# First FFN blocks in one written order: product 5 in halves around product 6, banks taken in turn, the next block's first product inside the down product

## The chip, the cores and the metric

One core of a Trainium2 chip runs the kernel. The metric is the device time of one execution in microseconds (us). The engines: PE is TensorE (matmuls), DVE is VectorE, ACT is ScalarE, POOL is GpSimd, SP is SyncE, which issues the loads. Each has its own queue of instructions and waits for semaphores of the others.

## The reference

One layer on x (512 rows, width 1024) and a memory of 256 rows, all in float32:

```
x = x + 1/2 * SwiGLU(RMSNorm(x))                       # FFN1: d_ff 2816
h = RMSNorm(x)
A, B, C = columns of h @ W_in:
   A: differential attention, 4 heads, rotary, block-causal
   B: chunked band attention, 8 heads, own chunk + 8 before, relative bias
   C: cross-attention into the memory:
      mk, mv = split(RMSNorm(mem) @ W_mem_kv)          # 256 x 512 each
      mk = RMSNorm per head(mk); cq = RMSNorm per head(cq)
      o_c = softmax(cq mk^T / sqrt(128)) mv
y = sum_i sigmoid(h W_g + b_g)_i * (o_i W_branch_i)
x = x + y W_out
x = x + 1/2 * SwiGLU(RMSNorm(x))                       # FFN2
x = RMSNorm(x)
SwiGLU(h) = (silu(h @ wg) * (h @ wu)) @ wd
```

## The kernel before

Each float32 product is made of three matmuls on operands split into a high part (a cast on ACT, L77, tiles with `hi` or `h` at the end) and a low part (a subtraction on DVE, L78, `lo` or `l`): high x high, low x high, high x low.

An FFN runs over the 22 tiles of d_ff in blocks of 4, 6, 6 and 6 (`CHUNKS`, L39). Within a block an `Item` is a pair of tiles. Its gate and up product for two tiles and two halves of the rows are computed by seven products instead of eight, in the manner of Strassen and Winograd: product p multiplies one of seven combinations of the four weight blocks (`prep`, L390) with one of seven combinations of the activations (`M[1]` to `M[7]`, made by `Operands.combine` and `need`, L205 to L242). A product is 24 matmuls of 256 columns (`mm7`, L364: two parts j, four k, three pairs of high and low). Products 1, 6, 7 and 4 add up in a bank of PSUM with the tag "s", products 5 and 3 in one with "p" or "o", product 2 has a bank "g". After products 1, 6 and 7 the state of the "s" bank is copied by ACT (`snap`, L417), since the next product of that chain adds to the same bank; `plus` (L422) adds such a copy to another bank on DVE (tile `cc`), `gated` makes silu(gate) x up (tile `pr`, L433), and `done` splits `pr` into `gh` and `gl`, the operands of the down product.

The weight combinations are DVE subtractions (`quarter` from `wraw`, L399, L400, L405, L409); `block` splits each into a ring of six buffer pairs: four `whi`/`wlo` and the two pairs `fhi`/`flo` and `ohi`/`olo`. So DVE and ACT make an operand pair for each product, while the first block also makes the seven activation operands (`mhi`/`mlo`).

After the products of a block comes its down product, in two halves of the columns (dh = 0 and 1); each has four banks, one for each 128 rows, and nf/2 pieces of 24 matmuls of 512 columns (`mm3`, L110 to L112). The last two products of the block, 4' and 3', stand between the first and the second piece of dh 0. (A prime stands for a block's second item.)

What sets the order: `run_jobs` (L334) prepares jobs ahead by a ring of six and runs each job's matmuls in a schedule of its own for PE; a scheduler places the jobs, and everything on DVE, ACT, POOL and SP. In the first block the order asked for is 1, 2, 1', 2', 6, 5, 7, 4, 3, 6', 5', 7', then the first down piece, 4', 3'. What PE got can be seen in the change's section.

Between the FFNs the mixer runs. Its cross-attention part makes the memory's keys: a product in two banks "s", a norm per head (`norm4`, with `mk` in L602) and transposes in bank "t" (`heads_T`, L615) into `mkh`/`mkl`; then `cq`, and then the values `mv`, again in two banks "s" (L651). In the mixer `PLAN_C0` and its likes are written rows that mix the steps of attention with pieces of other products. The banks in all: s 2, g 2, p 1, o 1, t 2 (L54).

## Time and profile before

| | us |
|---|---|
| median of 3 timed runs | 1266.1 (1265.81 to 1266.46) |
| the profiled execution | 1268.73 |
| its span | 1266.9 |
| PE busy | 1228.1 (97%) |
| DVE busy | 843.0 (67%) |
| ACT busy | 596.8 (47%) |
| PE in the chain that ended last | 91% |

The times of rows below are of the profiled execution, counted from the start of its span. Busy shares over the span hide stages; each row is read from the stage where it stands. The granted clock (PEclk) of 1.00 is 2.4 GHz, 0.50 is 1.2 GHz.

### The profile page before, as it was taken

The numbers are of one execution on the slowest core, as the hardware profiler recorded it, in microseconds if no ns is written. First come the engines' busy times: TensorE is split into PE (matmuls) and PEld (weight loads), VectorE is DVE, ScalarE is ACT, GpSimd is POOL, SyncE is SP. The second block draws the span as 40 slices with busy tenths as digits, with TensorE's granted clock in tenths as the row PEclk, the third lists the DMA queues.
The fourth block names the chain that finished last, engine by engine and source line by source line (L and its number), as shares of the span: only waits on it lengthen the run. The fifth ranks groups of instructions, "written<-read, shape, count | busy, mean of one in ns | idle before, by whom it ended". The sixth has DMA issues, their size and how long they took to land.

```text
span 1266.9 us, 19640 instructions
## 1 busy us (share of the span) xinstructions
PE 1228.1 (97%) x7808; PEld 1119.2 (88%) x7808; DVE 843.0 (67%) x1377; ACT 596.8 (47%) x1115; POOL 106.2 (8%) x108
## 2 busy tenths in 40 slices
PE   7889999999999899999999999999989999999997
PEld 7779989989987799999999999888887998998996
DVE  7977667667664756667765664554697776766753
ACT  7534525435443455554554544442464452542543
POOL 1100000000000301111121121111000000000002
PEclk8899999999999899999999999999989999999999
DMA  6532423323333413212221321145143242332311
GB/s 222 174 103 82 135 84 107 127 79 122 102 123 117 123 39 109 88 42 84 88 88 54 93 88 38 63 146 186 34 135 115 70 134 97 101 125 76 123 44 67
DMA packets 53084, 127.57 MB, mean 101 GB/s; under 512 B 10112, under 2 KB 10624, under 8 KB 52992
## 3 DMA queue, kind: packets, MB, share of 16 engines
q1 hardware_dynamic: 52416, 125.27, 31.1%
q8 instruction: 61, 1.00, 0.3%
q10 hardware_dynamic: 576, 1.05, 0.2%
q14 instruction: 31, 0.25, 0.1%
HBM read 122.11 MB, written 4.19 MB: 100 GB/s over the span
## 4 chain that ended last, share of the span: by engine, by line
PE 91%; DVE 4%; ACT 1%; DMA 1%; POOL 1%; issue 1%; SPq 0%; POOLq 0%; DVEq 0%; ACTq 0%
PE ps_s L373 19%; PE ps_g L110 9%; PE ps_g L112 9%; PE ps_g L111 9%; PE ps_o L373 5%; PE ps_p L110 5%; PE ps_p L112 5%; PE ps_p L111 4%; PE ps_p L373 4%; PE ps_g L373 4%; PE ps_s L110 3%; PE ps_s L111 3%; PE ps_s L112 3%; PE ps_o L906 2%; PE ps_s L874 2%; PE ps_t L722 1%
## 5 line engine op out<-in xcount | busy, mean ns | idle before, releaser
L77 ACT CAST whi<-wraw 128x1024 fp32r<-128x1024 f32 (+1 forms) x120 | 119.1, 993 | 144.6 <-PE ps_s L373 74.1
L78 DVE TENSOR_TENSOR wlo<-wraw,whi 128x1024 fp32r<-128x1024 f32 (+1 forms) x120 | 137.9, 1151 | 67.8 <-ACT whi L77 65.1
L373 PE MATMUL ps_s<-mhi,whi 128*128 128x256 f32 x496 | 140.3, 283 | 8.1 <-ACT snap L417 7.9
L373 PE MATMUL ps_s<-mlo,whi 128*128 128x256 f32 x496 | 139.3, 281 | 0.0
L373 PE MATMUL ps_s<-mhi,wlo 128*128 128x256 f32 x496 | 138.3, 281 | 0.6 <-DVE wlo L78 0.6
L373 PEld LDWEIGHTS ps_s<-mhi,whi 128*128 128x128 f32 x496 | 94.6, 191 | 10.6 <-ACT snap L417 9.5
L77 ACT CAST whi<-quarter 128x1024 fp32r<-128x1024 f32 x54 | 56.8, 1052 | 96.4 <-PE ps_o L112 22.4
L373 PEld LDWEIGHTS ps_s<-mlo,whi 128*128 128x128 f32 x496 | 94.7, 191 | 0.9 <-DVE mlo L78 0.2
L373 PEld LDWEIGHTS ps_s<-mhi,wlo 128*128 128x128 f32 x496 | 94.5, 191 | 0.9 <-DVE wlo L78 0.8
L110 PE MATMUL ps_p<-whi,hh 128*128 128x384 f32 (+1 forms) x264 | 95.0, 360 | 0.0
L112 PE MATMUL ps_p<-whi,hl 128*128 128x384 f32 (+1 forms) x264 | 89.6, 340 | 0.0
L111 PE MATMUL ps_p<-wlo,hh 128*128 128x384 f32 (+1 forms) x264 | 89.0, 337 | 0.0
L78 DVE TENSOR_TENSOR wlo<-quarter,whi 128x1024 fp32r<-128x1024 f32 x54 | 66.0, 1222 | 23.9 <-ACT whi L77 23.9
L110 PE MATMUL ps_g<-hh,fh 128*128 128x512 f32 x192 | 78.1, 407 | 0.0
L112 PE MATMUL ps_g<-hh,fl 128*128 128x512 f32 x192 | 75.5, 393 | 0.1
L111 PE MATMUL ps_g<-hl,fh 128*128 128x512 f32 x192 | 74.9, 390 | 0.0
L859 DVE CAST kx<-ps_t 128x256 fp32r<-128x256 f32 x32 | 13.6, 425 | 84.6 <-PE ps_t L857 84.6
L121 POOL TENSOR_TENSOR rsh<-msh,mhalf 128x4 f32<-128x4 f32 x38 | 45.2, 1191 | 277.5 <-DVE msh L127 225.8
L78 DVE TENSOR_TENSOR fl<-wraw,fh 128x768 fp32r<-128x768 f32 x48 | 50.0, 1042 | 24.0 <-ACT fh L77 24.0
L77 ACT CAST fh<-wraw 128x768 fp32r<-128x768 f32 x48 | 39.9, 833 | 37.7 <-PE ps_g L111 22.4
L724 ACT COPY pT<-ps_t 128x512 f32<-128x512 f32 (+3 forms) x56 | 23.5, 452 | 69.3 <-PE ps_t L722 69.3
L110 PEld LDWEIGHTS ps_p<-whi,hh 128*128 128x128 f32 x264 | 50.4, 191 | 1.6
(416 smaller groups left out, 3691.7 us busy)
## 6 DMA issues: line engine op xcount, KB each, us to landing
wraw<-in_ffn_w SPq DMA_DIRECT2D x88, 512.0 KB, 3.8
wraw<-in_ffn_wd SPq DMA_DIRECT2D x44, 512.0 KB, 3.9
wraw<-in_w_u SPq DMA_DIRECT2D x32, 384.0 KB, 3.2
wraw<-in_w_gb SPq DMA_DIRECT2D x32, 384.0 KB, 3.1
wraw<-in_w_gf SPq DMA_DIRECT2D x16, 384.0 KB, 3.1
wraw<-in_w_mem_kv SPq DMA_DIRECT2D x8, 512.0 KB, 4.1
wraw<-in_w_out SPq DMA_DIRECT2D x8, 512.0 KB, 4.8
x_sb<-in_x SPq DMA_DIRECT2D x4, 512.0 KB, 7.0
```

The costliest lines, as they stand in the source:

```text
L77: nc.scalar.copy(out=hi, in_=raw)
L78: (engine or nc.vector).tensor_tensor(out=lo, in0=raw, in1=f32(hi), op=ALU.subtract)
L110: nc.tensor.matmul(ps, lhsT=st[0], rhs=mv[0], start=first, stop=False)
L111: nc.tensor.matmul(ps, lhsT=st[0], rhs=mv[1], start=False, stop=False)
L112: return nc.tensor.matmul(ps, lhsT=st[1], rhs=mv[0], start=False, stop=last)
L121: nc.gpsimd.tensor_tensor(out=rs, in0=ms, in1=mhalf[:, :n], op=ALU.pow)
L373: nc.tensor.matmul(ps[:, c], lhsT=x, rhs=y, start=first and j + k + n == 0, stop=k == 3 and n == 2, skip_group_check=True)
L722: nc.tensor.transpose(ps[:, j * P:(j + 1) * P], pt[:, j * P:(j + 1) * P], ident)
L724: nc.scalar.copy(out=pT[:, :n * P], in_=ps[:, :n * P])
L859: nc.vector.tensor_copy(out=un.kx[:, :, qs], in_=heads(p2[:, 0:256], 2))
L874: nc.tensor.matmul(out_, lhsT=q, rhs=k, start=j == 0, stop=j == 1)
L906: nc.tensor.matmul(o[:, vs], lhsT=pT[:, j * P:(j + 1) * P], rhs=un.v[:, j, vs], start=j == 0, stop=j == i)
```

## The change

Both FFNs' first block gets one written order for PE. `run_jobs` opens one schedule for PE around all jobs of an FFN instead of one for each job, so that PE's matmuls stand in exactly the order of the list, over the blocks too. In the first block the list is now 1, 2, 1', 2', 5a, 6, 5b, 7, 6', 4, 3, 5', 7': product 5 is made in two halves (parts j = 0 and 1) around product 6. `prep` makes `s1` when the first of the products 5 and 6 needs it and `s4` after both. The first product of the second block is put at `hole`, after the products 4' and 3' within the first block's down product; the other blocks keep their lists. For dh = 1 the banks are taken in the order z, g, g, s instead of s, z, g, g. `G` (`gh`, `gl`) is made at its first use.

In the memory part the transposes of `mk` stand behind the product and the copies of `mv`, whose banks are "t" instead of "s"; `mk`, `mksq` and `cqsq` get tags of their own; `PLAN_C0` changes. `middle` is an argument that no call gives.

```
@@ run_jobs
-        for n, job in enumerate(jobs):
-            while made < len(jobs) and (made <= n or alive + jobs[made].blocks <= ring):
-                alive += jobs[made].blocks
-                jobs[made].got = jobs[made].prep() if jobs[made].prep else None
-                made += 1
-            with tc.manual_schedule(engines={mybir.EngineType.PE}):
+        with tc.manual_schedule(engines={mybir.EngineType.PE}):
+            for n, job in enumerate(jobs):
+                while made < len(jobs) and (made <= n or alive + jobs[made].blocks <= ring):
+                    alive += jobs[made].blocks
+                    jobs[made].got = jobs[made].prep() if jobs[made].prep else None
+                    made += 1
                 job.run(job.got)
-            alive -= job.blocks
+                alive -= job.frees
...
-        def mm7(ps, blk, m, first):
-            for j in range(2):
+        def mm7(ps, blk, m, first, parts=(0, 1)):
+            for j in parts:
...
+                if self.s1 is None:
+                    self.s1 = quarter()
+                    add(out=self.s1, in0=self.raw(2), in1=self.raw(3), op=ALU.add)
                 if p == 6:
-                    self.s1, self.s2 = quarter(), quarter()
-                    add(out=self.s1, in0=self.raw(2), in1=self.raw(3), op=ALU.add)
+                    self.s2 = quarter()
                     add(out=self.s2, in0=self.s1, in1=self.raw(0), op=ALU.subtract)
-                    return block(self.s2)
-                if p == 5:
-                    got = block(self.s1)
-                    self.s4 = quarter()
-                    add(out=self.s4, in0=self.raw(1), in1=self.s2, op=ALU.subtract)
+                    got = block(self.s2)
+                elif p == 5:
+                    got = self.blk5 = block(self.s1)
+                if p in (5, 6):
+                    self.done56 += 1
+                    if self.done56 == 2:
+                        self.s4 = quarter()
+                        add(out=self.s4, in0=self.raw(1), in1=self.s2, op=ALU.subtract)
                     return got
...
+                elif p == "5a":
+                    self.z = bank("p" if self.ft // 2 % 2 else "o")
+                    mm7(self.z, blk, 5, True, (0,))
+                elif p == "5b":
+                    mm7(self.z, self.blk5, 5, False, (1,))
...
+                order += [(items[0], "5a"), (items[0], 6), (items[0], "5b"), (items[0], 7), (items[1], 6), (items[0], 4),
+                          (items[0], 3), (items[1], 5), (items[1], 7)]
...
+                if n == 1:
+                    jobs.insert(hole, product(items[0], 1))
+                else:
+                    order += [(items[0], 1)]
...
-                    acc.extend(bank(t) for t in (("g", "g", "s", other) if dh == 0 else ("s", z, "g", "g")))
+                    acc.extend(bank(t) for t in (("g", "g", "s", other) if dh == 0 else (z, "g", "g", "s")))
...
                         if dh == 0 and k == 0:
                             jobs += end
+                            hole = len(jobs)
...
     for t in range(NMT):
-        yn = mem_pool.tile([P, 512], F32, tag="mk", name="mk", bufs=3)
-        sq = mem_pool.tile([P, 512], F32, tag="mk", name="mksq", bufs=3)
-        heads_T(norm4(mk_ps[t], yn, sq, gck), mkT, slice(t * P, (t + 1) * P))
+        yn = mem_pool.tile([P, 512], F32, tag="mk", name="mk", bufs=2)
+        sq = mem_pool.tile([P, 512], F32, tag="mksq", name="mksq", bufs=2)
+        mk.append(norm4(mk_ps[t], yn, sq, gck))
...
-    mv_ps = rows_product([bank("s") for _ in range(NMT)], mT, a["w_mem_kv"], 512, **mem_w)
+    mv_ps = rows_product([bank("t") for _ in range(NMT)], mT, a["w_mem_kv"], 512, **mem_w)
...
         nc.scalar.copy(out=mv[:, t, :], in_=mv_ps[t])
+    for t in range(NMT):
+        heads_T(mk[t], mkT, slice(t * P, (t + 1) * P))
...
-PLAN_C0 = "p2 c.qt p2 c.sc p2 f4 c.sc2 p3 f2 c.qt f2 c.pt f4 c.pv"
+PLAN_C0 = "p6 c.qt p3 f4 c.sc f4 c.sc2 f2 c.qt f1 c.pt f1 c.pv"
```

The first place is DVE in FFN1's first block. Before, with `flo_443` the low part of the operand of 6':

```order
L78 TENSOR_TENSOR mlo_65<-gl_126,mhi_64 128x1024
L141 SCALAR_TENSOR_TENSOR xn_3927<-mt_3917,rs_3925,gain_3888 128x512 x2
L78 TENSOR_TENSOR wlo_321<-quarter_318,whi_320 128x1024
L78 TENSOR_TENSOR wlo_361<-wraw_268,whi_360 128x1024
L399 TENSOR_TENSOR quarter_434<-wraw_436,wraw_438 128x1024
L78 TENSOR_TENSOR wlo_397<-quarter_282,whi_396 128x1024
L400 TENSOR_TENSOR quarter_435<-quarter_434,wraw_252 128x1024
L409 TENSOR_TENSOR quarter_509<-wraw_252,wraw_436 128x1024
L78 TENSOR_TENSOR olo_476<-quarter_434,ohi_475 128x1024
L422 TENSOR_TENSOR cc_543<-ps_o_483,snap_541 128x512
L405 TENSOR_TENSOR quarter_479<-wraw_258,quarter_435 128x1024
L78 TENSOR_TENSOR flo_443<-quarter_435,fhi_442 128x1024
```

In the changed kernel the low part for 6' is `wlo_361`:

```order
L439 TENSOR_TENSOR pr_424<-sg_425,cc_422 128x256
L78 TENSOR_TENSOR mlo_65<-gl_126,mhi_64 128x1024
L156 TENSOR_SCALAR ms_3638<-ss_3634 128x1
L78 TENSOR_TENSOR wlo_318<-quarter_315,whi_317 128x1024
L141 SCALAR_TENSOR_TENSOR xn_3642<-mt_3632,rs_3640,gain_3603 128x512 x2
L400 TENSOR_TENSOR quarter_352<-wraw_353,wraw_355 128x1024
L403 TENSOR_TENSOR quarter_358<-quarter_352,wraw_252 128x1024
L415 TENSOR_TENSOR quarter_491<-wraw_252,wraw_353 128x1024
L78 TENSOR_TENSOR olo_474<-quarter_352,ohi_473 128x1024
L411 TENSOR_TENSOR quarter_477<-wraw_258,quarter_358 128x1024
L428 TENSOR_TENSOR cc_523<-ps_o_434,snap_521 128x512
L78 TENSOR_TENSOR wlo_361<-quarter_358,whi_360 128x1024
```

Of the kernel before, `wlo_361` and `wlo_397`, the low parts for products 4 and 3, stand ahead of the low part for 6'. In the changed kernel they have left this place (product 4's follows behind, product 3's is a `flo` shortly ahead of this piece), and `pr` and `ms` have moved with the rows around them.

The second place is PE around the end of product 7 in FFN1's first block. Before, `ps_p_667` is 5', `ps_s_286` the first item's chain, here its products 7 (`whi_320`) and 4 (`whi_360`):

```order
L373 MATMUL ps_s_286<-mlo_65,whi_320 128x256
L373 MATMUL ps_s_286<-mhi_64,wlo_321 128x256
L373 MATMUL ps_p_667<-mhi_64,ohi_475 128x256
L373 MATMUL ps_p_667<-mlo_65,ohi_475 128x256
L373 MATMUL ps_s_286<-mhi_64,whi_360 128x256
L373 MATMUL ps_s_286<-mlo_65,whi_360 128x256
L373 MATMUL ps_s_286<-mhi_64,wlo_361 128x256
```

In the changed kernel `ps_s_284` with `whi_317` is product 7 and `ps_s_364` with `whi_360` product 6':

```order
L373 MATMUL ps_s_284<-mlo_65,whi_317 128x256
L373 MATMUL ps_s_284<-mhi_64,wlo_318 128x256
L373 MATMUL ps_s_364<-mhi_64,whi_360 128x256
L373 MATMUL ps_s_364<-mlo_65,whi_360 128x256
L373 MATMUL ps_s_364<-mhi_64,wlo_361 128x256
L373 MATMUL ps_s_364<-mhi_64,whi_360 128x256
L373 MATMUL ps_s_364<-mlo_65,whi_360 128x256
```

Where two matmuls of 5' and then product 4 followed product 7, product 6' follows it.

The third place is PE in the memory part. Before, `ps_s_4428` and `ps_s_4429` are the product for `mv`, and the transposes of the first `mk` (L615) stand between the two banks:

```order
L110 MATMUL ps_s_4428<-mwh_4450,mh_3886 128x512
L111 MATMUL ps_s_4428<-mwl_4451,mh_3886 128x512
L112 MATMUL ps_s_4428<-mwh_4450,ml_3887 128x512
L615 MATMUL ps_t_4232<-ident_80,mk_4221 128x128 x4
L110 MATMUL ps_s_4429<-mwh_4432,mh_3886 128x512
L111 MATMUL ps_s_4429<-mwl_4433,mh_3886 128x512
```

In the changed kernel the product for `mv` is in `ps_t_4129` and `ps_t_4130`, and the transposes (L638) of both `mk` and of the first `cq` (in `y_sb`) stand behind it:

```order
L110 MATMUL ps_t_4130<-mwh_4187,mh_3601 128x512
L111 MATMUL ps_t_4130<-mwl_4188,mh_3601 128x512
L112 MATMUL ps_t_4130<-mwh_4187,ml_3602 128x512
L638 MATMUL ps_t_4206<-ident_80,mk_3936 128x128 x4
L638 MATMUL ps_t_4213<-ident_80,mk_3947 128x128 x4
L638 MATMUL ps_t_4307<-ident_80,y_sb_4082 128x128 x4
L110 MATMUL ps_p_4286<-whi_4279,hh_3596 128x384
```

Three groups of transposes, in bank "t" as the product ahead of them, stand in a row.

## Rows read from the trace of the kernel before

**Rows 1.** Busy time by windows: us, then PE, PEld, DVE, ACT, POOL, clock, DMA, GB/s.

```profile
30.00:40.00 10.00, 5.67 (x27) 4.60 (x26) 9.56 (x12) 5.40 (x9) 4.86 (x1) 0.70 0.35 106
40.00:50.00 10.00, 8.46 (x57) 8.05 (x57) 9.56 (x12) 6.29 (x10) 1.39 (x1) 0.84 0.52 173
930.00:940.00 10.00, 9.68 (x63) 9.47 (x62) 10.00 (x12) 4.79 (x6) 0.00 (x0) 0.75 0.50 159
```

**Rows 2.** Waits of PE: releaser, us in total, times, longest.

```profile
PE ps_s L373 <- ACT snap L417: 7.9, 8, 1.5
PE ps_s L110 <- DVE mk L602: 5.8, 1, 5.8
...
PE ps_o L373 <- DVE mlo L78: 3.5, 2, 3.2
```

**Rows 3.** Busy time by windows, columns as in rows 1: stretches at half clock.

```profile
33.95:40.75 6.80, 5.16 (x21) 4.49 (x22) 6.36 (x9) 2.23 (x5) 0.93 (x1) 0.50 0.26 78
47.60:51.00 3.40, 3.40 (x18) 3.40 (x17) 3.40 (x4) 1.05 (x1) 0.00 (x0) 0.50 0.63 225
412.85:419.60 6.75, 4.68 (x11) 3.78 (x12) 4.72 (x10) 1.20 (x2) 2.60 (x3) 0.50 0.48 164
928.25:935.05 6.80, 6.20 (x29) 6.20 (x30) 6.80 (x9) 3.72 (x6) 0.00 (x0) 0.50 0.43 145
```

**Rows 4.** PE by time: start, us, line, operation, [idle before, releaser].

```profile
38.12 0.58 PE L373 MATMUL ps_o<-mlo,whi 128*128 128x256 f32 x1 [0.36 <-DVE mlo L78]
...
47.04 0.39 PE L373 MATMUL ps_s<-mhi,wlo 128*128 128x256 f32 x1 [0.62 <-DVE wlo L78]
...
414.92 0.77 PE L110 MATMUL ps_s<-mwh,mh 128*128 128x512 f32 x1 [5.78 <-DVE mk L602]
...
928.85 0.58 PE L373 MATMUL ps_o<-mlo,whi 128*128 128x256 f32 x1 [3.17 <-DVE mlo L78]
```

**Rows 5.** DVE by time, columns as in rows 4: first FFN, first block.

```profile
34.91 1.42 DVE L141 SCALAR_TENSOR_TENSOR xn<-mt,rs,gain 128x512 f32<-128x512 f32 x2 [0.44 <-POOL rs L121]
36.24 0.68 DVE L422 TENSOR_TENSOR cc<-ps_g,snap 128x512 f32<-128x512 f32 x1
36.84 1.22 DVE L78 TENSOR_TENSOR mlo<-gh,mhi 128x1024 fp32r<-128x1024 f32 x1
37.98 0.42 DVE L433 TENSOR_TENSOR pr<-sg,cc 128x256 f32<-128x256 f32 x1
...
40.05 1.22 DVE L78 TENSOR_TENSOR mlo<-gh,mhi 128x1024 fp32r<-128x1024 f32 x1
...
42.65 0.21 DVE L156 TENSOR_SCALAR ms<-ss 128x1 f32<-128x1 f32 x1
...
44.44 1.42 DVE L141 SCALAR_TENSOR_TENSOR xn<-mt,rs,gain 128x512 f32<-128x512 f32 x2 [0.44 <-POOL rs L121]
```

**Rows 6.** DVE by time: second FFN, first block.

```profile
921.30 1.22 DVE L78 TENSOR_TENSOR flo<-wraw,fhi 128x1024 fp32r<-128x1024 f32 x1
```

**Rows 7.** Chain that ended last, by time: start, us, what.

```profile
80.14 1.23 DVE wlo L78
...
84.14 0.50 PE ps_g L110
...
95.66 0.23 PE ps_g L111
...
100.98 2.83 PE ps_g L373 x24
...
989.31 0.71 PE ps_g L373 x6
```

**Rows 8.** ACT by time: middle, memory part.

```profile
424.91 1.28 ACT L643 ACT_TABLE_LOAD   x1
...
430.72 0.59 ACT L651 COPY mv<-ps_s 128x512 f32<-128x512 f32 x1 [1.60 <-PE ps_s L112]
...
432.33 1.57 ACT L77 CAST fh<-wraw 128x768 fp32r<-128x768 f32 x2
```

More of the change, by code (lines that the diff above doesn't have):

```diff
@@ L328, in layer_kernel, with __init__, ffn @@
     class Job:
[L331 to L332 removed]
+        def __init__(self, prep, run, blocks=1, frees=1):
+            self.prep, self.run, self.blocks, self.frees = prep, run, blocks, frees
     def run_jobs(jobs, ring):
         made = alive = 0
[L337 to L342 removed]
+        with tc.manual_schedule(engines={mybir.EngineType.PE}):
[4 more added lines that the diff above has]
+                    made += 1
                 job.run(job.got)
[L344 to L346 removed]
+                alive -= job.frees
+    def ffn(pre, x_sb, ops, fp, after, raws=None, before_last=None, after_half=None, middle=None):
         M = ops.M
@@ L382, in __init__ @@
                 self.pr = [None, None]
+                self.s1, self.done56 = None, 0
             def raw(self, i):
@@ L435, in done @@
             def done(self, f):
+                if not self.G:
+                    self.G += [fp.tile([P, 6, S], F32R, tag=t, name=t) for t in ("gh", "gl")]
                 split(self.pr[f], *(v[:, self.g0 + f, :] for v in self.G))
@@ L466, in product @@
         def product(item, p):
+            if p == "5a":
+                return Job(lambda: item.prep(5), lambda blk: item.run(p, blk), 1, 0)
+            if p == "5b":
+                return Job(None, lambda blk: item.run(p, blk), 0, 1)
             return Job(lambda: item.prep(p), lambda blk: item.run(p, blk))
         ft = 0
+        jobs = []
         for n, nf in enumerate(CHUNKS):
             last = n == len(CHUNKS) - 1
-            G = [fp.tile([P, 6, S], F32R, tag=t, name=t) for t in ("gh", "gl")]
+            G = []
             items = [Item(ft + i, G, i, raws if ft + i == 0 else None) for i in range(0, nf, 2)]
@@ L475, in ffn @@
             order = []
-            if ft == 0:
+            if n == 0:
                 order += [(items[0], 1), (items[0], 2), (items[1], 1), (items[1], 2)]
-            else:
-                order += [(items[0], 1), (items[0], 2)]
-            for i, item in enumerate(items):
-                order += [(item, 6), (item, 5), (item, 7)]
-                if i + 1 < len(items) and not (ft == 0 and i == 0):
-                    order += [(items[i + 1], 1)]
-                if ft == 0 and i == 0:
-                    order += [(item, 4), (item, 3)]
-                elif i + 1 < len(items):
-                    order += [(item, 4), (item, 3), (items[i + 1], 2)]
-            jobs = [product(*o) for o in order]
+                order += [(items[0], "5a"), (items[0], 6), (items[0], "5b"), (items[0], 7), (items[1], 6), (items[0], 4),
+                          (items[0], 3), (items[1], 5), (items[1], 7)]
+            else:
+                if n == 1:
+                    jobs.insert(hole, product(items[0], 1))
+                else:
+                    order += [(items[0], 1)]
+                order += [(items[0], 2)]
+                for i, item in enumerate(items):
+                    order += [(item, 6), (item, 5), (item, 7)]
+                    if i + 1 < len(items):
+                        order += [(items[i + 1], 1), (item, 4), (item, 3), (items[i + 1], 2)]
+            jobs += [product(*o) for o in order]
+            if n == 1 and middle:
+                jobs.append(Job(middle, lambda got: None, 0, 0))
             end = [product(items[-1], 4), product(items[-1], 3)]
```

11 lines of the change are left out of this document (4 added, 7 removed).

## The prediction

> **What bounds the kernel now.** The first view is the busy time by windows. In the opening of the first FFN the row of VectorE (DVE) stands at 9.56 and 9.56 of 10 us, while TensorE (PE) fills 5.67 and 8.46; in the opening of the second FFN DVE is at 10.00 [rows 1]. The reader is to see that in these two places DVE ends last and PE lives from what DVE releases. Everywhere between, PE is the bound and an edit is worth what it does to PE's waits.
>
> The second view is the waits of PE: 7.9 us in eight waits for ScalarE's (ACT) copy `snap`, which two products in one bank need between them; one wait of 5.8 us for `mk` in the middle; 3.5 us, nearly all in one wait, for `mlo` in the second FFN [rows 2]. The third is what a wait does afterwards. Four stretches have a granted clock of 0.50, 1.2 instead of 2.4 GHz [rows 3]. PE had just resumed at 38.12, 47.04, 414.92 and 928.85 [rows 4] and ran 2.6, 4.0, 4.7 and 6.2 us before the clock came back. At half clock a matmul with 256 columns takes 6.20 / 29 = 0.214 us, at full clock 2.83 / 24 = 0.118 [rows 3, 7], so 0.45 of the busy time is lost: of 5.16, 3.40, 4.68 and 6.20 that is 2.3, 1.5, 2.1 and 2.8, a mean of **2.2 us for each drop**.
>
> **The first FFN's first block.** Count of matmuls, operand splits and DMAs is unchanged; product 5 in two pieces has the same 24. What counts is the order. A step of DVE, start to start, is 1.14 for 128x1024 (36.84 to 37.98) and 0.60 for 128x512 (36.24 to 36.84), which is the busy time less 0.08 of overlap; by the same rule 0.34 for `pr`, 0.13 for `ms` and 1.34 for a pair of `xn` [rows 5].
>
> *DVE.* Up to the split that ends at 34.47, where DVE idles 0.44 until 34.91 [rows 5], both orders hold the same work. The new order puts the low part of operand 5 there, from 34.39 (0.08 of overlap), done 35.6 (36.84 + 1.22 = 38.06 before), and one block split (`flo`) more before the low part of operand 7; in exchange the 0.44 of idling is filled. Operand 7's split starts at 40.05 + 1.14 - 0.44 = 40.75, that of operand 6's second half 0.60 before it. From there the rows of the changed order give: operand 7, L415, operand 4 and block 7 (4 x 1.14), `pr` 0.34, `ms` 0.13, a wait for `rs` of 0.44 as at 44.44 now, `xn` 1.34, then L400, L403, L415, `olo`, L411 (5 x 1.14) and `cc` 0.60. So `wlo` of the second item's product 6 starts at 40.75 + 4.56 + 0.34 + 0.13 + 0.44 + 1.34 + 5.70 + 0.60 = 53.86 and ends 1.22 later, at **55.1**.
>
> *PE.* 5a starts at 35.6 (its first matmul, as before, is issued earlier); the 11 others at half clock take 2.3 and the eight transposes 1.9 to 2.3: 40.2. Product 6 waits for its operand until 40.8, ends at 43.5; 5b, 1.4, ends at 44.9 and covers the copy `snap` for which product 7 waited before. Product 7 waits for block 7's low part, 44.63 + 1.22 = 45.85, and ends at 48.4. Now comes the second item's product 6. In the kernel before, its place was taken by product 5 of the second item and product 4 of the first, whose operands were there. Written order forbids that: PE issues two matmuls and stands until 55.1, **6.7 us**, with products 4, 3, 5' and 7' queued behind. Then 2.5 for the rest of 6', four products of 2.76 to 2.83 = 11.0, and 24 matmuls of 512 columns at 0.23 [rows 7], 5.5, for the first down piece: 74.1. Products 4', 3' and the next block's first, 8.3: 82.3. The second down piece needs `gh` and `gl` of the second item. Before, that chain after the last covered matmul ran from 80.14 to 84.14, 4.0 us [rows 7]; here it begins when 3' ends, and the moved product covers 2.8 of it; with one more 128x1024 split ahead of `gl` the wait is 4.0 - 2.8 + 1.1 = 2.3, at most 4.0, at least nothing. So 84.6, and three pieces of 5.45 (24 x 0.23 before rounding) give 100.9 for the start of the next block's second product, against 100.98 in the trace [rows 7]. All that the new order covers is given back in the one wait: -0.1. The clock is the rest: a wait of 6.7 is longer than the four that were followed by half clock, so I add one drop: **+2.1**. Ends: -0.1 if no drop comes or the second wait absorbs it, +3.5 if the second wait has one too.
>
> PE's matmuls run one behind the other: when 928.85 had to wait 3.17, nothing overtook it [rows 4]. The Trainium skill, page "TensorE: Matmul & The Clock Gate", section "Part 2: What happens when you issue a matmul", says that only weight loads are pulled ahead and matmuls stay in program order. This rule speaks against the change, and the trace agrees; if matmuls could pass a waiting one, products 4 and 3 would fill 5.6 of the 6.7 us and the sum would be some 5 us lower.
>
> **The second FFN's first block.** Same orders, other norms. Ahead of the split of the second item's product 2 (`flo`, 921.30 [rows 6]) DVE now also has the low part of block 6, L415 and L236, and a step of 1.14 less from the first item's block: +2.0, so 923.3. `flo`, `olo`, L238 (3 x 1.14), `cc` 0.60 and one `mlo` 1.14 later operand 5's low part starts at 928.46 and is done at 929.7; before, PE resumed on it at 928.85 [rows 4]. Three steps of 1.14, operand 6's half and `cc` (2 x 0.60), three of 1.14, `pr`, four of 1.14 and `pr` lead on to product 6': 928.46 + 3.42 + 1.20 + 3.42 + 0.34 + 4.56 + 0.34 = 941.7, done 942.9. On PE product 2' waits until 924.5 (2.8), 5a until 929.7 (2.5), 6 until operand 6's half at 932.5 (1.5) and runs to 935.2, 5b and 7 to 939.3, and 6' waits 3.6. With 2.5 for its rest, 11.0, 5.5, 8.3, a wait of 2.2 and 16.35 as above the next block's second product starts at 988.7 against 989.31 [rows 7]: -0.6 at full clock. One drop was there already [rows 3]; the new row of waits of over 2 us has two to three. I take 1.5 more: **+2.7**, ends -0.6 and +3.8.
>
> **The middle.** The 5.78 us wait goes [rows 4]: the product for `mv` gets bank "t" and needs no `mk`, and the row of transposes stands behind it. What is late next: both transposes of `mk` and the first of `cq` need bank "t" again. The first waits for the copy of `mv` (0.59, ACT), the third for cast and split of the first `mk`. Between these ACT has the table load 1.28, a copy 0.59, two `fh` 1.57 and the cast 0.59 [rows 8], DVE a split of 0.60; 4.6 less the 1.15 of matmuls after the first bank's end = 3.5, and 0.7 for the smaller waits: 4.2. A drop of 2.1 stood behind the old wait; 3.5 is in the class that had one. So 4.2 - 5.8 = -1.6, and 0.5 for the changed PLAN_C0 row: **-1.1**; ends -3.3 (no drop either) and +1.5 (7.3 for all waits, if `fl` holds the first split too).
>
> **What costs nothing or little.** The order of banks in the second half's down product lets the next block begin in another bank. The rows of before show no wait there but those of `snap`, of which one was at most 1.5 and the mean 1.0 [rows 2]; for the few transitions +0.5, ends -0.5 and +2. The moved product's `wraw` load goes ahead of three `wd` loads in SP's queue; the DMA share of 0.35 and 0.52 [rows 1] leaves the room that hides it, and without that a piece of 5.45 would wait for a load by less than that +2. `G` made late, separate tags for `mksq` and `cqsq`: memory alone, hidden, 0; a conflict of buffers would cost a step of DVE, 0.6.
>
> **Sum.** +2.1 + 2.7 - 1.1 + 0.5 = +4.2. The profiled execution took 1268.73 (span 1266.9 and 1.83 around it), 2.6 over the median of the timed runs, 1266.1; the difference is applied to the median: **1270.3**. Ends: -0.1 - 0.6 - 3.3 - 0.5 = -4.5 and +3.5 + 3.8 + 1.5 + 2 = +10.8.
>
> Beside it, by a page: the Trainium skill's "TensorE: Matmul & The Clock Gate", section "Terms", prices throttled time at itself times (1 - K/N). Half of the four stretches (23.75) is 11.9, 3.0 a drop instead of 2.2; with 2.5 added drops the sum would be 2 higher. Rows 3 show idle time inside two of the stretches, so the trace agrees with the form but not with the whole size.
>
> **Rivals.**
> 1. *DVE is not what 6' waits for* (faster). If its low part is there when 7 ends, PE keeps 6.7 and 3.6 us and two drops of 2.2: 1270.3 - 14.7 = **1255.6**. The 7.9 of `snap` waits speak for it. Against it: DVE at 9.56 to 10.00 [rows 1], and thirteen-odd steps before 55.1. It decides once 6' starts before some 50. 12%.
> 2. *No drops beyond those of before*: 1270.3 - 2.2 - 3.3 = **1264.8**, no change. For it: only four stretches at half clock stand beside the eleven waits of rows 2. Against it: the two longest waits, 5.78 and 3.17, each had one [rows 3, 4]. 20%.
> 3. *Each wait over 2 us brings a drop*: two in the first FFN, four less one in the second, 5 x 2.2 - 0.7 = +10.3, and +1.5 + 0.5: **1278.4**. 13%.
> 4. *It does not do what it says*: the first product moves only between blocks one and two, so three of four transitions keep their order; already in the sum, and no time of its own.
>
> **Chances.** The forecast's case has 55%, its own range 1267 to 1275. About 2.5 us, 0.2%, is what a measurement can tell from none. Of the forecast's 55 points 12 lie within that of 1266.1 and 1 on the faster side; of rival 2's 20 points 13 lie within, 5 faster, 2 slower. Same 12 + 13 = 25%, faster 12 + 1 + 5 = 18%, slower 42 + 2 + 13 = 57%. The range reaches from the lower end, 1261.8, to rival 3: 1261 to 1279, which leaves out rival 1 and part of 3.
>
> **What would show it.** In the new profile: a PE wait of 6 to 7 us for `wlo` near 48 to 55, the granted clock at 0.50 behind it; waits for `snap` down from 7.9 to near 2; the `mk` wait gone and one for `mkl` or a bank of "t" of 3 to 4 near 420; 3.4 us near 940. Wrong if 6' follows 7 without a gap, or if the clock stays whole behind that gap.

## The result and the profile after

The changed kernel takes 1278.07 us, the median of four runs (1276.82 to 1279.74), against 1266.10 for the kernel before, the median of three: a ratio of 1.0095, 95% interval 1.0075 to 1.0115. A fourth execution of the kernel before took 1740.59, in the slow state, and is left out. It is slower, as forecast, and inside the range of 1261 to 1279, but by 12 us and not by 4, and outside the 1267 to 1275 of the forecast's own case. The profiled execution took 1278.56, its span is 1276.7, so 9.8 us of the profiled span is there to be found in the two traces. It lies so, between places where both kernels have done the same work; the last two columns say how much of each change is idle time and how much busy time of PE:

| stage | before | after | change | PE idle | PE busy |
|---|---|---|---|---|---|
| start to the second block's second product, FFN1 | 101.0 | 106.3 | +5.3 | +4.1 | +1.2 |
| from there, over the end of FFN1, to the memory's first product | 295.0 | 296.5 | +1.4 | 0.0 | +1.4 |
| memory part and first mixer steps | 55.8 | 53.5 | -2.3 | -1.2 | -1.1 |
| mixer, to FFN2's first transposes waited for | 460.2 | 460.0 | -0.2 | -0.5 | +0.3 |
| from there to FFN2's second block, second product | 77.4 | 80.7 | +3.3 | +3.3 | 0.0 |
| from there to the end | 277.6 | 279.8 | +2.2 | +0.9 | +1.4 |

The first and the fifth line end at these pieces of the chain of waits after (start, us, what), which answer to the rows 100.98 and 989.31 of [rows 7]:

```profile
106.29 2.83 PE ps_g L373 x24
...
996.92 2.83 PE ps_g L373 x24
```

The waits of PE after (releaser, us in total, times, longest):

```profile
PE ps_s L373 <- DVE wlo L78: 6.8, 3, 3.3
...
PE ps_o L373 <- DVE mlo L78: 4.8, 2, 3.9
PE ps_g L110 <- ACT gh L77: 4.0, 2, 2.0
PE ps_s L373 <- ACT whi L77: 2.8, 1, 2.8
PE ps_s L373 <- DVE mlo L78: 2.7, 4, 1.2
PE ps_t L638 <- DVE mkl L78: 2.6, 1, 2.6
PE ps_g L373 <- DVE flo L78: 2.6, 1, 2.6
...
PE ps_t L638 <- ACT mv L675: 1.1, 1, 1.1
```

`snap` (7.9 before) and `mk` (5.8) are gone, as [rows 2] shows them; in their place stand operands: `wlo`, `whi`, `mlo` and `flo` of the first blocks, `gh` ahead of the second down piece, and `mkl` and `mv` in the memory part. By the page's first part (busy time, share of the span, instructions of PE) PE is idle for 1276.7 - 1231.3 = 45.4 us, against 1266.9 - 1228.1 = 38.8 before, and busy 3.2 longer with the same instructions:

```profile
PE 1231.3 (96%) x7808; PEld 1120.2 (88%) x7808; DVE 846.1 (66%) x1377; ACT 598.6 (47%) x1115; POOL 109.1 (9%) x108
```

PE by time in FFN1's first block (start, us, line, operation, idle before and its releaser):

```profile
35.60 0.58 PE L373 MATMUL ps_o<-mlo,ohi 128*128 128x256 f32 x1 [3.88 <-DVE mlo L78]
...
41.27 0.39 PE L373 MATMUL ps_s<-mlo,whi 128*128 128x256 f32 x1 [1.03 <-DVE mlo L78]
...
46.27 0.39 PE L373 MATMUL ps_s<-mhi,wlo 128*128 128x256 f32 x1 [0.43 <-DVE wlo L78]
...
51.83 0.39 PE L373 MATMUL ps_s<-mhi,whi 128*128 128x256 f32 x1 [2.76 <-ACT whi L77]
...
55.66 0.58 PE L373 MATMUL ps_s<-mhi,wlo 128*128 128x256 f32 x1 [3.33 <-DVE wlo L78]
...
87.88 0.65 PE L110 MATMUL ps_g<-ohi,gh 128*128 128x512 f32 x1 [2.02 <-ACT gh L77]
```

These are 5a, product 6, product 7, 6' twice (its `whi`, its `wlo`), and the second down piece. 6' stands 2.76 + 3.33 us. Behind it and behind the second down piece the granted clock is at 1.2 GHz, which the windows at half clock show (columns as in [rows 1]); in FFN1's block the first answers to the first of [rows 3], the two others stand in place of the one at 47.60; one stands in the memory part and two in FFN2:

```profile
33.30:40.15 6.85, 4.54 (x20) 4.23 (x20) 6.41 (x8) 3.65 (x6) 2.66 (x1) 0.51 0.21 73
53.90:60.70 6.80, 5.04 (x23) 5.04 (x24) 5.45 (x6) 1.18 (x3) 0.00 (x0) 0.50 0.83 276
88.00:91.45 3.45, 3.45 (x8) 2.39 (x9) 2.42 (x4) 0.00 (x0) 0.00 (x0) 0.51 0.02 5
436.15:439.55 3.40, 2.71 (x10) 2.71 (x11) 2.02 (x5) 0.59 (x1) 2.06 (x4) 0.51 0.95 103
931.25:934.65 3.40, 2.89 (x14) 2.60 (x13) 3.40 (x4) 3.40 (x5) 0.00 (x0) 0.51 0.01 2
948.20:951.60 3.40, 3.33 (x15) 3.33 (x16) 3.40 (x5) 0.00 (x0) 0.00 (x0) 0.50 0.85 266
```

PE is busy for 21.96 us in these stretches and for 19.44 in the four of [rows 3]. At 0.45 of the busy time, the prediction's price, the 2.52 more cost an estimated 1.1 us. So of the 9.8 us most, 6.6, is idle time, little is the clock, and some 2 are busy time at full clock.

FFN2's first block: the waits ahead of 2', 5a, 6, 6' and the second down piece:

```profile
929.91 0.39 PE L373 MATMUL ps_g<-mhi,flo 128*128 128x256 f32 x1 [2.60 <-DVE flo L78]
...
935.04 0.39 PE L373 MATMUL ps_o<-mlo,ohi 128*128 128x256 f32 x1 [0.90 <-DVE mlo L78]
...
937.92 0.39 PE L373 MATMUL ps_s<-mlo,whi 128*128 128x256 f32 x1 [1.19 <-DVE mlo L78]
...
948.27 0.58 PE L373 MATMUL ps_s<-mhi,wlo 128*128 128x256 f32 x1 [3.06 <-DVE wlo L78]
...
979.77 0.50 PE L110 MATMUL ps_g<-ohi,gh 128*128 128x512 f32 x1 [2.02 <-ACT gh L77]
```

### The profile page after: what moved, and what is told of

Read it like the earlier page. It is cut to its first block, busy times and chain, and to the rows that moved or that the text cites. A ratio compares the mean times of both kernels' runs of the same rounds, so it can differ in the third digit from the quotient of the medians.

```text
span 1276.7 us, 19649 instructions
## 1 busy us (share of the span) xinstructions
PE 1231.3 (96%) x7808; PEld 1120.2 (88%) x7808; DVE 846.1 (66%) x1377; ACT 598.6 (47%) x1115; POOL 109.1 (9%) x108
## 4 chain that ended last, share of the span: by engine, by line
PE 89%; DVE 5%; DMA 2%; ACT 1%; POOL 1%; issue 1%; SPq 0%; POOLq 0%; DVEq 0%; ACTq 0%
PE ps_s L373 18%; PE ps_g L110 9%; PE ps_g L112 9%; PE ps_g L111 9%; PE ps_o L373 5%; PE ps_p L110 5%; PE ps_p L112 5%; PE ps_p L111 5%; PE ps_p L373 4%; PE ps_g L373 4%; PE ps_s L112 2%; PE ps_s L110 2%; PE ps_s L111 2%; PE ps_o L932 2%; PE ps_s L900 2%; PE ps_t L748 1%
## 5 line engine op out<-in xcount | busy, mean ns | idle before, releaser
L373 PE MATMUL ps_s<-mhi,wlo 128*128 128x256 f32 x512 | 145.2, 284 | 6.8 <-DVE wlo L78 6.8
L373 PE MATMUL ps_s<-mhi,whi 128*128 128x256 f32 x512 | 145.3, 284 | 2.8 <-ACT whi L77 2.8
L373 PE MATMUL ps_s<-mlo,whi 128*128 128x256 f32 x512 | 145.0, 283 | 2.7 <-DVE mlo L78 2.7
L373 PEld LDWEIGHTS ps_s<-mhi,wlo 128*128 128x128 f32 x512 | 98.9, 193 | 7.4 <-DVE wlo L78 7.4
L373 PEld LDWEIGHTS ps_s<-mhi,whi 128*128 128x128 f32 x512 | 99.2, 194 | 3.5 <-ACT whi L77 3.0
L373 PEld LDWEIGHTS ps_s<-mlo,whi 128*128 128x128 f32 x512 | 98.4, 192 | 4.3 <-DVE mlo L78 3.9
L78 DVE TENSOR_TENSOR wlo<-quarter,whi 128x1024 fp32r<-128x1024 f32 x54 | 66.0, 1223 | 38.8 <-ACT whi L77 38.8
L121 POOL TENSOR_TENSOR rs<-ms,mhalf 128x1 f32<-128x1 f32 x18 | 17.2, 957 | 419.4 <-DVE ms L156 355.7
```

Of the source, the lines that this page charges most:

```text
L78: (engine or nc.vector).tensor_tensor(out=lo, in0=raw, in1=f32(hi), op=ALU.subtract)
L121: nc.gpsimd.tensor_tensor(out=rs, in0=ms, in1=mhalf[:, :n], op=ALU.pow)
L373: nc.tensor.matmul(ps[:, c], lhsT=x, rhs=y, start=first and j + k + n == 0, stop=k == 3 and n == 2, skip_group_check=True)
```

## The experiments

Ratios are of the runs of each kernel to the runs of the kernel before on the same chip, with 95% intervals. Where a kernel adds or leaves out work, the text says so.

**late6.** In both first blocks 6' behind products 4 and 3.

```
-  (items[0], 7), (items[1], 6), (items[0], 4), (items[0], 3),
+  (items[0], 7), (items[0], 4), (items[0], 3), (items[1], 6),
```

> The changed kernel, but in both FFNs' first block the second item's product 6 stands behind the first item's products 4 and 3 (7, 4, 3, 6', 5', 7'). Theory 1 (the place of 6' in the written order is what costs): after 7 ends near 49, product 4 has its operands and fills 2.8 us of the 6.1 that PE waits ahead of 6' now; product 3 then waits some 3 to 4 us for the sum cc on DVE. The next block's second product starts 2 to 4 us earlier in each FFN than in the changed kernel: 1271 to 1274 against 1278. Rival 2 (DVE's total of work sets the end of the block, so the wait only moves): 1276 to 1279, and the wait reappears ahead of the second down piece. Rival 3 (the order was right and half clock is all that costs): the 0.50 stretch stays behind product 3's wait, 1277.

1.0099 (1.0084 to 1.0114): nothing won. FFN1 gained 2.3, its second block's second product at 104.0, but PE then waited ahead of the first down piece:

```profile
68.01 0.50 PE L110 MATMUL ps_g<-whi,gh 128*128 128x512 f32 x1 [2.02 <-ACT gh L77]
...
69.47 0.67 PE L112 MATMUL ps_g<-whi,gl 128*128 128x512 f32 x1 [0.72 <-DVE gl L78]
```

and in FFN2 the waits ahead of 5a and 6 became 2.23 and 2.98 with a half-clock stretch of 10.2 us from 933.2 on, and the second block's second product, 2.0 ahead when FFN2 began, is 1.8 behind: 3.9 lost. In FFN1's block the listed waits from product 6 to the second down piece are 9.1 us in all against 9.6 in the changed kernel, so the 2.3 go with the clock more than with the waits: one half-clock stretch of 3.4 us behind the first down piece in place of the two behind 6' and the second. Rival 2 holds here: the place of 6' moves the wait, it does not remove it. Theory 1, that this place decides, fell.

**mem.** The kernel before with the change of the memory part alone.

```
-  mk_ps ... heads_T(norm4(...)) within the loop;  mv in bank("s")
+  mk.append(norm4(...));  mv in bank("t");  heads_T behind the copies of mv;  new PLAN_C0
```

> The kernel before with the change in the memory part alone (transposes of mk behind the product and the copies of mv, mv in banks t, own tags, the new PLAN_C0). Theory 1 (the middle is a gain that the FFNs hide): between the same places around the memory part the changed kernel's trace is 6.75 late ahead of it and 4.46 late behind it, 2.3 won, so 1264 (1263 to 1265). Rival (that difference comes from where the FFN's end leaves the queues and not from this part): 1266 or more.

1.0011 (1.0002 to 1.0019): no gain, a trace of a loss. The stage took 55.7 against 55.8. PE was idle 0.8 less in it, but the clock fell twice here, once behind a wait for `mwl` (1.88), which the changed kernel has too (1.54) without a fall behind it, and once at the transposes (columns as in [rows 1]):

```profile
411.00:419.00 8.00, 6.12 (x20) 4.56 (x20) 8.00 (x17) 3.50 (x5) 5.24 (x5) 0.79 0.73 236
431.80:435.20 3.40, 3.40 (x12) 3.02 (x11) 2.18 (x8) 1.12 (x3) 1.99 (x5) 0.51 0.90 232
```

The changed kernel's trace has one such stretch in this part (3.4 us long), so a part of its -2.3 hangs on the clock. The 0.4 us that mem's trace is longer than before's stand in FFN2's first block (78.8 us against 77.4), which the edit doesn't touch.

**filler.** The changed kernel with matmuls whose results are not used, 52 in FFN1 and 24 in FFN2, ahead of 6'.

```
+  if self.ft == 2:
+      pad = bank("p")
+      for i in range(52 if pre == "ffn1" else 24):
+          nc.tensor.matmul(pad[:, :HS], lhsT=M[1][0][:, i % 4, :P], rhs=M[1][0][:, i % 4, :], start=True, stop=True)
   mm7(self.y, blk, 6, False)
```

> The changed kernel with matmuls added that compute nothing that is used: 52 with 256 columns ahead of 6' in FFN1's first block and 24 in FFN2's, into a bank that is overwritten later. They take 5.9 and 2.7 us, which PE would wait anyway (6.1 and 3.06). Theory 1 (half clock behind the waits costs 2.3 us in FFN1 and 1.6 in FFN2 at 6'): the stretches of 0.50 near 54 to 61 and 948 to 952 go, and the time falls by about 3 to 4, to 1274 to 1275. Rival 2 (DVE sets the end of the block whatever the clock): the stretches go and the time stays at 1277 to 1279. Rival 3 (the clock falls anyway): the stretches stay.

1.0086 (1.0071 to 1.0100), not told apart from the changed kernel's 1.0095. The stretch behind 6' went, the clock is at 2.4 GHz there:

```profile
54.00:61.00 7.00, 6.86 (x60) 6.65 (x59) 6.56 (x7) 2.45 (x4) 0.00 (x0) 1.00 0.78 264
```

and FFN1's first block ended 2.1 earlier (104.0), the 2.3 that theory 1 gave less 0.2. In FFN2 the stretch behind 6' went as well, but one stood behind the second down piece from 981.0, and the later blocks of both FFNs ran 3.2 and 3.3 us longer than before. In FFN1 that takes back most of the gain, at the second down pieces of the second and third block, where PE now waits for `gh`:

```profile
171.76 0.50 PE L110 MATMUL ps_g<-whi,gh 128*128 128x512 f32 x1 [0.69 <-ACT gh L77]
...
264.21 0.50 PE L110 MATMUL ps_g<-whi,gh 128*128 128x512 f32 x1 [0.95 <-ACT gh L77]
```

The price of a drop is shown in its place; that it can be won back for the whole is not. The Trainium skill, page "TensorE: Matmul & The Clock Gate", section "Terms", would price the stretch behind 6' at half its 6.80 us, 3.4; the 2.1 that were won lie nearer to 0.45 of PE's 5.04 busy in it, 2.3.

**whole5.** Product 5 whole.

```
-  (items[0], "5a"), (items[0], 6), (items[0], "5b"), (items[0], 7),
+  (items[0], 5), (items[0], 6), (items[0], 7),
```

> The changed kernel with product 5 whole ahead of 6 (5, 6, 7, 6', 4, 3, 5', 7') instead of in halves around it. Theory 1 (PE has 6.1 us of slack ahead of 6', so nothing that comes before it decides): 6' resumes at the same 55.7, time 1277 to 1279, the same. Rival (the halves are a cost or a gain of their own, by the copy snap they cover or the clock at 5a): product 7 waits 0.6 to 1.5 for snap and the time rises by that, or falls by 2 as the half-clock stretch near 33 to 40 is spread differently.

1.0075 (1.0062 to 1.0089), a little under the changed kernel, with intervals that overlap. 6' resumed at 55.68 (55.66 with halves) although product 7 now waited 0.86 for `snap`: PE's slack ahead of 6' takes up whatever is before it, as theory 1 says. What FFN1 gained (1.8 us) came from the clock: behind 6' it was back at 59.7 instead of 60.7, and no stretch followed the second down piece.

**loose.** The changed kernel with a schedule for each job, as before.

```
-        with tc.manual_schedule(engines={mybir.EngineType.PE}):
-            for n, job in enumerate(jobs):
...
+            with tc.manual_schedule(engines={mybir.EngineType.PE}):
+                job.run(job.got)
```

> The changed kernel with everything as it is, but each job again in a schedule of its own, so that PE's jobs may be interleaved where the scheduler finds one ready, as in the kernel before. Theory 1 (the strictly written order of PE is what costs: it pins 6' ahead of products that are ready, pins 4' and 3' behind the first down piece, and holds up the later blocks by 1.5 and 2.2 us): 1266 to 1270, near the kernel before. Rival 2 (the lists, halves and the moved product cost, whoever places them): 1274 to 1279. Rival 3 (the banks and the memory part): 1274 or more too, with the first block as fast as before.

1.0028 (1.0019 to 1.0036), at the upper end of theory 1's range: of 12 us 8 are won back with lists, halves, banks, moved product and memory part all in place. The execution that was profiled, 1267.73, is the fastest of the twelve, so its rows show this kernel at its best. PE's waits hold neither `gh` nor `flo` any more and `wlo` once with 1.7; the longest rows are (columns as above):

```profile
PE ps_t L201 <- DVE xn L141: 4.8, 2, 3.3
PE ps_s L373 <- ACT snap L423: 4.1, 4, 1.5
PE ps_o L373 <- ACT mhi L77: 2.8, 1, 2.8
```

**strict.** The kernel before, its own lists, but one schedule for PE over all jobs of a block. (Its `run_jobs` is called once for each block, so this is not yet one schedule for an FFN, as the expectation has it.)

```
+        with tc.manual_schedule(engines={mybir.EngineType.PE}):
             for n, job in enumerate(jobs):
...
-            with tc.manual_schedule(engines={mybir.EngineType.PE}):
-                job.run(job.got)
+                job.run(job.got)
```

> The kernel before with its own lists, banks and memory part, but one schedule for PE around all jobs of an FFN, so that its matmuls stand in the listed order. Theory 1 (the written order alone costs a good part): 1271 to 1277; waits of 2 to 4 us ahead of the second down piece, since 4' and 3' stand behind the whole first piece, and 1 to 2 us more in the later blocks of each FFN. Rival (the order before was nearly the listed one, and the lists and the moved product cost): 1266 to 1269.

1.0168 (1.0151 to 1.0184), 21 us, more than theory 1 gave. Ahead of the first down piece and within it PE waits for `gh` and `gl`, ahead of the second for `gh`:

```profile
68.10 0.50 PE L110 MATMUL ps_g<-whi,gh 128*128 128x512 f32 x1 [2.02 <-ACT gh L77]
...
70.37 0.79 PE L112 MATMUL ps_g<-whi,gl 128*128 128x512 f32 x1 [1.54 <-DVE gl L78]
...
87.74 0.79 PE L110 MATMUL ps_g<-fhi,gh 128*128 128x512 f32 x1 [3.86 <-ACT gh L77]
```

In all 12.5 us for `gh` where the kernel before has 0.5. Of the 20.7 us between the two traces 10.6 are idle time of PE and 10.1 busy time, most of the latter at half clock. With loose this settles the main cause: the written order. It costs the old list 21 us and the new one 8; without it what is left of the change costs 3.5.

**nohole.** The changed kernel with the next block's first product at its former place.

```
-                if n == 1:
-                    jobs.insert(hole, product(items[0], 1))
-                else:
-                    order += [(items[0], 1)]
-                order += [(items[0], 2)]
+                order += [(items[0], 1), (items[0], 2)]
```

> The changed kernel with the second block's first product at its former place, behind the down product. Theory 1 (the moved product covers part of the chain from 3' to the second down piece): without it PE waits some 3.9 instead of 2.02 ahead of that piece and does 2.8 of work later: 1.8 slower in each FFN, 1280 to 1283. Rival (the moved product makes the wait: its snap and the next cast into fhi stand ahead of the last gh in ACT's queue, and without it gh comes 2 us earlier): the wait of 2.02 goes to under 1 and the time to 1273 to 1276.

1.0139 (1.0124 to 1.0154): theory 1, and more. The wait is as long as was worked out:

```profile
87.06 0.50 PE L110 MATMUL ps_g<-fhi,gh 128*128 128x512 f32 x1 [3.86 <-ACT gh L77]
```

The moved product thus gives back some 5 us of what the written order takes.

**d0late.** 4' and 3' ahead of the first block's first down piece.

```
+                        if dh == 0 and k == 0 and n == 0:
+                            jobs += end
                         jobs.append(...)
-                        if dh == 0 and k == 0:
-                            jobs += end
+                        if dh == 0 and k == 0:
+                            if n:
+                                jobs += end
```

> The changed kernel with the first block's products 4' and 3' ahead of the first down piece instead of behind it (4', 3', first piece, the next block's first product, second piece). Theory 1 (the chain from 3' over gh to the second piece is too long for its cover of 2.8): the first piece now covers it with 5.45 more, the 2.02 us wait ahead of the second piece goes in both FFNs, with the half clock behind it where it came: 3 to 6 faster than the changed kernel, 1272 to 1275. Rival (the block ends when DVE ends, the order of pieces moves nothing): the wait moves ahead of 4' or the first piece, 1277 to 1279.

1.0072 (1.0057 to 1.0086), about 2.9 under the changed kernel, with intervals that overlap, and just under the 3 to 6 of theory 1. The wait of 2.02 ahead of the second piece went in both FFNs; one for `snap` came, since 4' now follows 7' in the same bank:

```profile
72.69 0.39 PE L373 MATMUL ps_s<-mhi,whi 128*128 128x256 f32 x1 [1.51 <-ACT snap L423]
```

**keepclock.** The kernel before with unused matmuls in two waits: 18 behind the product for `mk`, 24 ahead of FFN2's product 5.

```
+        if fill:
...
+                for _ in range(fill):
+                    nc.tensor.matmul(pad, lhsT=actT[0][:, 0, 0:P], rhs=wc[1][:, 0:512], start=True, stop=True)
...
-    mk_ps = rows_product([bank("s") for _ in range(NMT)], mT, a["w_mem_kv"], 0, **mem_w)
+    mk_ps = rows_product([bank("s") for _ in range(NMT)], mT, a["w_mem_kv"], 0, fill=18, **mem_w)
...
+        if self.ft == 0 and pre == "ffn2":
+            for i in range(24):
+                nc.tensor.matmul(self.z[:, :HS], lhsT=M[5][0][:, i % 4, :P], rhs=M[5][0][:, i % 4, :], start=True, stop=True)
         mm7(self.z, blk, 5, True)
```

> The kernel before with matmuls added that compute nothing that is used, in two of its waits: 18 with 512 columns behind the product for mk (4.1 us in the wait of 5.78) and 24 with 256 columns ahead of product 5 in FFN2's first block (2.7 us in the wait of 3.17). Theory 1 (the half clock behind a wait costs 2.1 and 2.8 us there, and PE rather than DVE ends those stages): the two 0.50 stretches go and the time falls by 3 to 5, to 1262 to 1264, below both kernels. Rival 2 (DVE sets the end of FFN2's block): only the 2.1 of the middle is won, 1264 to 1265. Rival 3 (the added matmuls delay what they stand ahead of, or the clock falls all the same): 1266 to 1268.

1.0018 (1.0009 to 1.0027): rival 3, a little above its range. Both old stretches are gone, but 12 us later a new wait and a new stretch stand in the memory part:

```profile
432.03 0.39 PE L110 MATMUL ps_g<-mkh,cqh 128*128 128x256 f32 x1 [1.96 <-ACT cqh L77]
...
433.60 0.58 PE L112 MATMUL ps_g<-mkh,cql 128*128 128x256 f32 x1 [1.07 <-DVE cql L78]
```

```profile
409.00:420.00 11.00, 9.70 (x43) 7.34 (x42) 9.39 (x17) 5.64 (x10) 2.06 (x3) 1.00 0.54 179
926.00:934.00 8.00, 7.72 (x66) 7.52 (x66) 8.00 (x9) 5.55 (x8) 0.00 (x0) 1.00 0.01 2
432.80:439.60 6.80, 6.00 (x18) 5.32 (x19) 2.08 (x6) 1.02 (x4) 3.08 (x6) 0.51 0.86 175
```

(The first fence is PE by time, the second has columns as in [rows 1].) The added matmuls changed where the scheduler put the transposes of `mk` and `cq`. In FFN2 the stage from the first transposes to the second block's second product took 76.8 against 77.4 before: the clock that was won there was worth 0.6, not 2.8. PE leads by 2.4 through the products and loses most of that ahead of and in the down product, where it now waits for `cc` (0.40 and 0.19) and `gh` (0.46) and before waited for neither. It is no version that beats the kernel before.

**oldbanks.** `("s", z, "g", "g")` again for the second half.

```
-  (z, "g", "g", "s")
+  ("s", z, "g", "g")
```

> The changed kernel with the banks of the second half's down product in the former order (s, z, g, g). Theory 1 (the 1.5 and 2.2 us that the later blocks of the FFNs lose come with the written order of PE, not with the banks): the same, 1277 to 1280, or 1 slower where a block's first product meets a bank that is still read. Rival (the banks' order is what the later blocks lose): 1274 to 1276.

1.0097 (1.0083 to 1.0111): the same as the changed kernel, as theory 1 says. The banks are worth nothing that can be measured here.

**d0whole.** The edits of d0late and of whole5 together.

```
+  (items[0], 5), (items[0], 6), (items[0], 7), ...
+  jobs += end      # n == 0: ahead of the first piece
```

> The changed kernel with both edits that made it faster alone: product 5 whole ahead of 6 (2.5 won) and 4' and 3' ahead of the first down piece (2.9 won). Theory 1 (they act at different waits): they add up, 1273 to 1275. Rival (both let PE run into the same wait ahead of 6', so one gain eats the other): 1276.

1.0063 (1.0050 to 1.0077). Less than the sum of both gains in the point values (1.0052 would be the sum), and its interval holds both expectations: not settled.

**firsttight.** The one schedule over the first block and the moved product alone.

```
+            if n < tight:
+                job.run(job.got)
+            else:
+                with tc.manual_schedule(engines={mybir.EngineType.PE}):
+                    job.run(job.got)
```

> The changed kernel with the one schedule only over the first block's jobs and the moved product; the later blocks' jobs each have their own again. Theory 1 (in the later blocks too the strict order is what costs, 1.5 us in the first FFN and 2.2 in the second): those stretches go back to 295.0 and 277.7 us, and the time falls by 3 to 4 to 1274 to 1275; the waits of the first block stay as they are. Rival (the later blocks lose it by the moved product or the banks): 1277 to 1279.

1.0061 (1.0049 to 1.0074), 4 us under the changed kernel, as theory 1 gave. The wait of 2.02 for `gh` is gone, because a product of the second block was let in ahead of the second down piece; what is left of it is a wait for `snap`:

```profile
87.85 0.39 PE L380 MATMUL ps_s<-mhi,whi 128*128 128x256 f32 x1 [1.50 <-ACT snap L430]
```

So the gain has two sources, the later blocks and this place. Compared where both traces have done equal work, the first blocks gain 1.7 and 2.7, the later blocks 1.1 and 1.0, and the memory part gives back 2.3, with two half-clock stretches in place of one. The 2.7 is in part the clock too: FFN2's block has one stretch, the changed kernel's two.

No kernel of these beats the kernel before.

## Why the prediction was right in its direction and too small

1. *DVE's chain, right.* 5a was to start at 35.6 and started at 35.60; product 6 at 40.8 (41.27), 7 on `wlo` at 45.85 (46.27), 6' at 55.1 (55.66). Counting the steps of one in-order queue from its start-to-start rows gave every release within 0.6 us over 20 us. In FFN2 the waits were to be 2.8, 2.5, 1.5 and 3.6 and are 2.60, 0.90, 1.19 and 3.06. The second down piece was to wait 2.3 and waits 2.02 in both FFNs.

2. *What the waits do to the clock, mis-sized in FFN1.* The term was +2.1: a chain that ended 0.1 under before's, one drop at 6' and none behind the second down piece. Its upper end was +3.5; measured is +5.3. Two stretches came, behind 6' (from 55.66, 5 us of work at half clock, 2.3 lost) and behind the second down piece (3.45 us, 1.6 lost), and 6' resumed 0.6 late. With the -0.1 that is 4.4; the rest is spread over the products and pieces behind 6', a little in each, and was not traced further. Two drops are rival 3's mechanism in FFN1, to which 13% was given; that its total of 1278.4 lies next to the measured 1278.07 is luck, since it holds +1.5 for the middle, where -2.3 came, and +0.5 for the later blocks. The range holds the result because it reaches up to that total. Compared with the kernel before, whose stretch at 47.60 is gone, the clock is the smaller part: PE is idle 4.1 longer in this stage and busy 1.2 longer. In FFN2 +2.7 was forecast, with 1.5 drops of 2.2 in it, and +3.3 measured. Two drops came, but of 2.89 and 3.33 us of work, so that together they cost what before's one of 6.20 cost; the 3.3 is all idle time.

3. *Why the second down piece waits, told too simply.* The price was right; half of the reason is in the order of ACT. The cast into `fhi`, for a later job, may only begin when PE has read that buffer for the moved product; `snap` and then the last `gh` stand behind it in the queue (ACT by time, columns as above):

```profile
85.78 1.04 ACT L77 CAST fhi<-quarter 128x1024 fp32r<-128x1024 f32 x1 [0.91 <-PE ps_s L373]
86.73 0.58 ACT L423 COPY snap<-ps_s 128x512 f32<-128x512 f32 x1
87.20 0.62 ACT L77 CAST gh<-pr 128x512 fp32r<-128x512 f32 x1
```

So the piece waits for the end of the product that was to cover it, and 1.04 + 0.58 + 0.62 less the overlaps. nohole, where `gh` is not behind that cast, shows the alternative: 3.86 without cover. There `gh` waits for `pr` alone and starts at 86.39; its trace runs 0.14 later here, so the cast's place in the queue makes 0.95 of the 2.02, and the chain through `pr` that was forecast makes the rest.

4. *The middle, right in sign and in its waits, its size in part luck.* -1.1 was forecast, -2.3 came, with the two waits foreseen near the transposes (4.2 forecast for all of them, 1.07 and 2.64 here, and 1.54 for `mwl`, 5.3 in all):

```profile
433.54 0.66 PE L638 MATMUL ps_t<-ident,mk 128*128 128x128 f32 x4 [1.07 <-ACT mv L675]
...
436.84 0.47 PE L638 MATMUL ps_t<-ident,y_sb 128*128 128x128 f32 x1 [2.64 <-DVE mkl L78]
```

Idle time fell by 1.2 and busy time by 1.1, the latter mostly by the clock: before's trace has a stretch of 6.8 us here (4.68 of work), the changed kernel's one of 3.4 (2.71). mem, the same edit with two of 3.4, wins 0.1. But the stage takes 55.8 and 56.0 in the two traces with the old memory part and nothing added (before, strict) and 53.2 to 54.7 in the changed kernel and the nine others built on it, so the edit does win here, 1 to 2.5 as the clock falls.

5. *The step that failed: "for the few transitions +0.5".* The later blocks lost 1.4 in each FFN; the 0.9 that is left of the table's last line stands behind the last matmul (7.6 us against 6.8; strict has 6.8 and nohole 6.7). The prediction treated the one schedule as a matter of the first block and of bank order. firsttight gives back 4 by freeing the later blocks and the place behind the moved product, oldbanks 0: it is the strict order. The lists of waits don't show how, since PE counts as busy throughout in both kernels (FFN1's later blocks, before and after, columns as in [rows 1]):

```profile
100.98:395.83 294.85, 294.85 (x2047) 273.10 (x2046) 199.15 (x239) 130.88 (x190) 2.19 (x4) 1.00 0.34 109
106.29:402.58 296.29, 296.25 (x2046) 273.35 (x2046) 201.32 (x240) 132.74 (x191) 2.20 (x4) 1.00 0.34 105
```

A row of the down product is 0.39 long and the next one starts 0.23 later, so a stall under 0.16 leaves no idle time. The starts show the stalls: at the second down piece of the second and third block PE comes to `gh` and `gl` too early, here by 0.2:

```profile
264.10 0.39 PE L112 MATMUL ps_o<-whi,gl 128*128 128x512 f32 x1
264.54 0.50 PE L110 MATMUL ps_g<-whi,gh 128*128 128x512 f32 x1
```

These stalls add up to 0.9 us in FFN1 and 0.8 in FFN2; the kernel before, loose and firsttight have none there, strict has 1.1 in FFN1. The rest, 0.6 in each FFN, is in the products of the slower kind (last section). More generally the prediction priced the list, while the experiments show that the schedule around it is the cost: strict, the old list in written order, is the slowest of all at 21 us over the kernel before, loose, the new list in free order, is within 4 of the kernel before. What hid this before was the filling: 4' and 3' between the matmuls of the first down piece, parts of 5' and 4 while an operand was late.

6. *The time of the profile against the median.* 2.6 us were taken off because the profiled execution of before lay so far over its median. After, it lay 0.5 over, so 2.1 of the 12 us are in no term of the sum.

7. *Slips that move no term.* The lower end of the sum is 1266.1 - 4.5 = 1261.6, not 1261.8, and 74.1 + 8.3 is 82.4. Three of the four stretches of [rows 3] hold idle time, not two (6.80 - 6.20 in the last). The trace of before has a fifth, from 13.5 to 20.3 in the opening, and there a wait of 3.25 for `xn`, longer than the 3.17 that was called one of the two longest; both kernels have these.

Rival 1 (DVE is not what 6' waits for) is out by the 3.33 us wait. Rival 2 (no further drops) is out by the stretches behind 6'.

## What to carry to other kernels

When several engines feed an in-order queue, count the feeding engine's steps first: where it is full, a new order of the fed engine can only move a wait. Writing an order out by hand also takes away the filling that a scheduler found; price that in every block the schedule reaches, not only where the list changed. And a buffer ring couples a late cast to the product that still reads its slot: what is queued behind that cast is late with it. Where a list of waits shows nothing, compare the starts: stalls of 0.2 us leave PE busy by its rows.

## What was not expected of the hardware

At an unchanged granted clock of 1.00 a product of 24 matmuls takes 2.83 us at the start of each block and 2.72 later (chain of waits of the changed kernel, start, us, what):

```profile
128.89 2.83 PE ps_s L373 x24
...
142.69 2.72 PE ps_p L373 x24
```

The slower kind lasts from 106 to 134 in the changed kernel and from 98 to 114 in the kernel before, in block 2, and comes back in each later block of both FFNs, for 22 to 30 us after and 16 to 25 before. In block 2 the 12 us more at 4% are half a us; what makes it was not found. Second, the same short wait is sometimes followed by a half-clock stretch and sometimes not: ahead of the same matmul 1.82 for `mwl` was in firsttight (a stretch from 420.3 to 423.7) and 1.82 was not in oldbanks (the clock at 1.00 from 419 to 425). The stretches behind waits of like length lasted from 3.4 us (the changed kernel from 948.2, behind 3.06) to 10.2 (late6 from 933.2, with waits of 2.23 and 2.98). Whether a single drop comes is not to be told ahead of the run, and it is as large as the differences between several of these kernels.
